# Placing the matmuls' moving operands modulo 256 bytes in a two-layer decoder trunk

## The chip, the cores and the metric

The kernel runs on one core of one Trainium2 chip. The metric is the device time of one execution in microseconds (us); lower is better. Profiles name the engines PE (matmul), PEld (weight load of PE), DVE (vector), ACT (scalar), POOL and SP (which here only issues DMAs). L402 means line 402 of the kernel before.

## What is computed

A decoder trunk of two layers over 528 tokens (512 and 16 meta tokens) of width 1024, in float32. Each layer is half a SwiGLU, a mixer (retention in layer 0, gated linear attention, GLA, in layer 1), and another half SwiGLU; a norm closes the trunk.

```
def swiglu(x, w_in, w_out):
    gate, up = jnp.split(x @ w_in, 2, axis=-1)
    return (jax.nn.silu(gate) * up) @ w_out
...
    for i in range(DEPTH):
        j = i // N_MIXERS
        h = h + 0.5 * swiglu(rmsnorm(h, norm_ffn1[i]), ffn1_w_in[i], ffn1_w_out[i])
        hn = rmsnorm(h, norm_mix[i])
        if i % N_MIXERS == 0:
            mix = retention(hn, ret_w_in[j], ret_head_norm[j], ret_w_out[j])
        else:
            mix = gla(hn, gla_w_in[j], gla_w_gate[j], gla_b_gate[j], gla_head_norm[j], gla_w_out[j])
        h = h + mix
        h = h + 0.5 * swiglu(rmsnorm(h, norm_ffn2[i]), ffn2_w_in[i], ffn2_w_out[i])
    h = rmsnorm(h, final_norm)
    return h[:, N_META:]
```

The hidden width of a SwiGLU is 2816, which is 22 tiles of 128.

## The kernel before

**Products.** Activations lie with the features on the 128 partitions and the tokens along the free axis. Every float32 operand is split in a rounded part `hi` and a rest `lo`, and a product is three matmuls (`mm3`, L402 to L404): weights `hi` with activations `hi`, weights `hi` with activations `lo`, weights `lo` with activations `hi`. The weights (`whi`, `wlo`) are the stationary operand, loaded afresh for each matmul by PEld; the activations are the moving operand, mostly 264 columns (half of the tokens), 256 in the last SwiGLU. In PE's order, a chunk k of 128 input features is three matmuls, with moving operands `hi`, `lo`, `hi`.

**Weights.** `Weights` streams all weights in one planned order: raw tiles by SP's DMA queue, sums of two of them with the help of POOL's, then a split on ACT (L160) and DVE (L161) into two tiles of 512 columns, 2048 bytes a partition, out of 14 in the pool `wsplit`. The split runs four tiles ahead of PE. A chunk k is 128 columns, 512 bytes. Retention has four more such tiles in a pool of its own, `wmore`.

**Units.** Most projections are done two output tiles and two halves of the tokens at a time as a unit (`unit_steps`) of seven passes in place of eight. Each pass multiplies one weight quarter (n chunks, four in the input projections; four or three in the output projections of the SwiGLUs) with one moving operand. In the usual order the moving operands are n11, t1, t2, n21, n3, n22, t4. In an input projection n11, n21 and n22 are slices of `uh` and `ul` (the scaled input, `hi` and `lo`, a tile of eight rows of 528 columns), and n3, t1, t2, t4 are the four quarters of `th` and `tl`, sums of the normed input, four per chunk, each 264 columns. In an output projection all seven lie in one hidden tile `h` per chunk, `hi` and `lo` each with seven slices of 264 columns, in the order n21, n22, n11, n3, t1, t2, t4. The hidden tiles rotate over four buffers (tag `H`).

```
            th, tl = [tp.tile([P, 4, 4, 264], F32R, tag=f"t{i}", name=f"t{i}{me}") for i in "hl"]
...
                    h = hp.tile([P, 2, 7, 264], F32R, tag="H", name=f"h{me}{f}")
...
                    og[h] = [rp.tile([P, 4, T], F32R, tag="v" + i, name=f"og{i}{h}") for i in "hl"]
```

**Memory.** All tiles lie in on-chip memory, one start address for all partitions. Pools are placed behind one another in the order in which they are opened: constants (`const`), the residual stream (`resid`), `upool` with `uh`, `ul` and the norm rows `rb` and `rc`, `tmp` with the scratch tiles, the three weight pools, and then whatever pools a stage opens: in a SwiGLU the hidden tiles, `th` and `tl`, and three scratch tiles; in retention one pool `rp`; in GLA one pool `gp`. A stage's pools are closed at its end, and the next stage's take their place, each tile when the last reader of what lay there is done.

**Norms.** `stats` (L524 to L537) sums the squares by matmul, raises the mean to the power -1/2 on POOL (L535, with a constant tile `half_neg` of eight columns), and `spread` brings the result to all partitions as `rb` (L546). Meanwhile PE runs the next stage's first plain projections, which need `uh` alone.

**Order.** A scheduler of the language sorts each engine's instructions by priority and expected readiness; the text's order decides between equals. The causal mask (`causal`, L356) and a copy of its corner at three places (`ctail`, L359) are used by retention alone.

Of the kernel before, what the change touches and what calls it, by code (L numbers as in the profile page):

```python
# [10 lines left out]
F32 = mybir.dt.float32  # L11
F32R = mybir.dt.float32r
# [40 lines left out]
PW = 512  # L53
AHEAD = 4
# [164 lines left out]
def trunk(ctx, tc, a):  # L219
# [6 lines left out]
    tmp = ctx.enter_context(tc.tile_pool(name="tmp", bufs=2))  # L226
    acc = ctx.enter_context(tc.tile_pool(name="acc", bufs=2, space=bass.MemoryType.PSUM))
    W = Weights(tc, ctx)

# [125 lines left out]
    causal = const.tile([P, P], F32, name="causal")  # L355
    nc.sync.dma_start(causal, a["tri"][1])  # L356
    ctail = const.tile([3 * MR, MR], F32, name="ctail")
    for g in range(3):
        S.copy(ctail[g * MR:(g + 1) * MR], causal[g * MR:(g + 1) * MR, g * MR:(g + 1) * MR])  # L359
# [7 lines left out]
    half_neg = const.tile([P, 8], F32, name="half_neg")  # L367
    V.memset(half_neg, -0.5)
# [6 lines left out]
    rb = upool.tile([P, T], F32, tag="rb", name="rb")  # L375
    rc = upool.tile([P, 8], F32, tag="rc", name="rc")
# [61 lines left out]
    def rsqrt_rows(sq, parts, width, name, finish):  # L438
# [10 lines left out]
        ms = tmp.tile([P, 8], F32, tag="ms", name=f"ms_{name}")  # L449
        V.tensor_scalar(ms[:w, :nj], st[:w, :nj], 1.0 / width, EPS, ALU.mult, ALU.add)  # L450
        r = tmp.tile([P, 8], F32, tag="r", name=f"r_{name}")
        G.tensor_tensor(r[:w, :nj], ms[:w, :nj], half_neg[:w, :nj], ALU.pow)
# [12 lines left out]
    def enter(gcol, by, lag=1, lag2=1):  # L465
# [52 lines left out]
        def stats():  # L518
# [12 lines left out]
            for (b0, w, nb, m), c in zip(by, cols):  # L531
                ms = tmp.tile([P, 8], F32, tag="ms", name=f"ms_{name}{c}")
                V.tensor_scalar(ms[:w, :nb], st[:w, c:c + nb], 1.0 / D, EPS, ALU.mult, ALU.add)
                r = rc[:w, c:c + nb]
                G.tensor_tensor(r, ms[:w, :nb], half_neg[:w, :nb], ALU.pow)  # L535
                n = m // nb
                ins = V.tensor_tensor(dg[:w, b0:b0 + m].rearrange("p (j t) -> p j t", j=nb),  # L537
                                      ident[:w, :n].unsqueeze(1).broadcast_to([w, nb, n]),
                                      r.unsqueeze(2).broadcast_to([w, nb, n]), ALU.mult)
# [102 lines left out]
    def quarters(halves, th, tl):  # L642

        tl = tl if isinstance(tl, list) else [tl[:, k] for k in range(4)]
        wd = width(halves)

        def rhs(what, k):
            if what in ("n11", "n21", "n22"):
                k, (r0, r1) = k + (4 if what[1] == "2" else 0), halves[int(what[2]) - 1]
                return uh[k][:, r0:r1], ul[k][:, r0:r1]  # L650
            i = ("n3", "t1", "t2", "t4").index(what)
            return th[:, k, i, :wd], tl[k][:, i, :wd]
# [4 lines left out]
    def ffn(which, layer, halves, gcol, feed, late=False):  # L657
# [5 lines left out]
        with tc.tile_pool(name=f"h_{me}", bufs=4) as hp, tc.tile_pool(name=f"t_{me}", bufs=1) as tp, \  # L663
                tc.tile_pool(name=f"u_{me}", bufs=3) as up_, psum_pool(4) as pp:
            other["pool"] = pp
            th, tl = [tp.tile([P, 4, 4, 264], F32R, tag=f"t{i}", name=f"t{i}{me}") for i in "hl"]
# [21 lines left out]
            def sums(j):  # L688
                norm(j)
                for i in range(2):  # L690
                    k = 2 * j + i
                    u_sums(up_, f"{me}{k}", halves, normed[j][:, i].rearrange("p h t -> p (h t)"), th[:, k], tl[:, k])
# [17 lines left out]
            def hidden(f, y, part=None):  # L710
# [15 lines left out]
                else:  # L726
                    h = hp.tile([P, 2, 7, 264], F32R, tag="H", name=f"h{me}{f}")
# [248 lines left out]
    def out_last(key, hh, hl, halves, scale):  # L976
# [80 lines left out]
        ms = tmp.tile([P, 8], F32, tag="ms", name="ms_fb")  # L1057
        V.tensor_scalar(ms[:, :2], st[:, :2], 1.0 / D, EPS, ALU.mult, ALU.add)
        r = tmp.tile([P, 8], F32, tag="r", name="r_fb")
        G.tensor_tensor(r[:, :2], ms[:, :2], half_neg[:, :2], ALU.pow)  # L1060
# [15 lines left out]
    def retention(feed):  # L1076
        with tc.tile_pool(name="retp", bufs=1) as rp, tc.tile_pool(name="wmore", bufs=2) as wp, psum_pool(4) as pp:
# [4 lines left out]
            th, tl = [rp.tile([P, 4, 4, 264], F32R, tag=f"t{i}", name=f"rt{i}") for i in "hl"]  # L1082
# [9 lines left out]
            def sums(k):  # L1092
# [7 lines left out]
                u_sums(rp, f"r{k}", HALVES, un.rearrange("p h t -> p (h t)"), th[:, k], tl[:, k])  # L1100
# [17 lines left out]
            def head(h):  # L1118
# [222 lines left out]
                def result():  # L1341

                    og[h] = [rp.tile([P, 4, T], F32R, tag="v" + i, name=f"og{i}{h}") for i in "hl"]
# [64 lines left out]
    def gla(feed):  # L1408
        with tc.tile_pool(name="glap", bufs=1) as gp, psum_pool(2) as pp, \
# [6 lines left out]
            th = gp.tile([P, 4, 4, 264], F32R, tag="th", name="gth")  # L1416
# [5 lines left out]
            def sums(k):  # L1422
# [16 lines left out]
                split(th[:, k, :2], tl[k][:, :2], t01)  # L1439
                split(th[:, k, 2:], tl[k][:, 2:], t23)  # L1440
# [641 lines left out]
```

## Time and profile before

| | |
|---|---|
| median of 3 runs | 2070.59 us (2070.3 to 2073.34) |
| the profiled execution's own time | 2071.41 us |
| its span, first to last instruction | 2069.6 us |
| granted TensorE clock | 0.999 |
| bytes read from main memory | 311.76 MB |
| DMA, mean over the span | 154 GB/s |

A row of the timeline has the start in us, the duration in us, the engine, the line, the operation, what it writes and reads, the shapes and the count. A matmul's duration is longer than the distance to the next one's start, since matmuls overlap; the pace of PE is read from starts. A row of a group has, behind the bar, the busy time and the mean duration in ns, then the idle time before it and what ended it. A row of the windows has the busy time and the count of each engine.

### The profile page before, as it was taken

The page shows a single profiled execution, that of the slowest core. Times are in us where ns is not written, and L with a number is a line of the kernel's source. Part 1 is how long each engine was busy: PE and PEld are TensorE (multiplying, and loading weights), DVE is VectorE, ACT ScalarE, POOL GpSimd, SP SyncE. Part 2 cuts the span into 40 slices and gives each one's busy share as a digit, 9 for nine tenths or more (in the row PEclk, how much of TensorE's full clock was granted, in tenths as well). Part 3 has the DMA queues.
Part 4 walks back from the last instruction along what each step waited for, and adds up shares of the span by engine and source line. Part 5 has one row for each costly group of instructions (what it writes and reads, how often), then busy time and mean ns, then how long its engine had stood idle before and what let it go on. Part 6 is the DMA issues. An engine that isn't in the chain of part 4 may idle for free.

```text
span 2069.6 us, 42946 instructions
## 1 busy us (share of the span) xinstructions
PE 2057.5 (99%) x16335; PEld 2012.9 (97%) x16335; DVE 1790.8 (87%) x3218; ACT 1200.2 (58%) x2365; POOL 208.8 (10%) x181
## 2 busy tenths in 40 slices
PE   9999999999999999999999999999999999999998
PEld 9999999999999999999999999999999988999998
DVE  8988889978686889988889998889897968998886
ACT  5756566554545455656666565666645445666664
POOL 1011111010101000111111011111001000111110
PEclk9999999999999999999999999999999999999999
DMA  7676777355555532776776476677614351687772
GB/s 224 154 193 158 193 185 185 107 144 132 146 132 138 136 104 70 184 191 158 195 188 172 111 180 179 162 197 177 194 57 119 91 165 61 161 214 174 183 179 72
DMA packets 176112, 318.84 MB, mean 154 GB/s; under 512 B 17569, under 2 KB 40737, under 8 KB 175905
## 3 DMA queue, kind: packets, MB, share of 16 engines
q1 hardware_dynamic: 133856, 237.04, 34.6%
q0 software_dynamic: 40896, 75.51, 23.5%
q10 hardware_dynamic: 1152, 3.55, 0.5%
q8 instruction: 128, 2.10, 0.4%
q14 instruction: 80, 0.65, 0.1%
HBM read 311.76 MB, written 4.26 MB: 153 GB/s over the span
## 4 chain that ended last, share of the span: by engine, by line
PE 95%; DVE 2%; ACT 1%; issue 1%; DMA 0%; POOL 0%; SPq 0%; POOLq 0%; ACTq 0%; DVEq 0%
PE po_r L403 2%; PE po_r L402 2%; PE po_r L404 2%; PE Xf20o L402 1%; PE Xf10o L402 1%; PE Xf11o L402 1%; PE Xf10o L404 1%; PE Xf10o L403 1%; PE Xf20o L403 1%; PE Xf20o L404 1%; PE Xf11o L403 1%; PE Xf11o L404 1%; PE lv L1614 1%; PE Xf20u L402 1%; PE Xf11u L402 1%; PE Xf21u L404 1%
## 5 line engine op out<-in xcount | busy, mean ns | idle before, releaser
L160 ACT CAST whi<-raw 128x512 fp32r<-128x512 f32 (+1 forms) x893 | 525.6, 606 | 482.3 <-DVE raw L166 92.2
L161 DVE TENSOR_TENSOR wlo<-raw,whi 128x512 fp32r<-128x512 f32 (+1 forms) x893 | 584.1, 669 | 143.8 <-ACT whi L160 134.7
L160 ACT CAST whi<-pair 128x512 fp32r<-128x512 f32 (+1 forms) x304 | 183.5, 604 | 122.2 <-PE Xf11u L403 7.3
L161 DVE TENSOR_TENSOR wlo<-pair,whi 128x512 fp32r<-128x512 f32 (+1 forms) x304 | 202.0, 664 | 6.4 <-ACT whi L160 5.0
L129 POOL DMA_DIRECT2D pair<-in_f_in x73 | 88.5, 1213 | 725.4 <-DVE wlo L161 313.6
L166 DVE TENSOR_TENSOR raw<-pair,raw 128x512 f32<-128x512 f32 (+1 forms) x146 | 97.3, 667 | 2.6
L168 DVE TENSOR_TENSOR raw<-raw,raw 128x512 f32<-128x512 f32 (+1 forms) x146 | 97.3, 666 | 2.5
L129 POOL DMA_DIRECT2D pair<-in_f_out x44 | 53.2, 1208 | 379.1 <-DVE wlo L161 208.8
L402 PE MATMUL po_r<-ogh,whi 128*128 128x264 f32 x256 | 73.0, 285 | 0.0
L403 PE MATMUL po_r<-ogl,whi 128*128 128x264 f32 x256 | 73.0, 285 | 0.0
L404 PE MATMUL po_r<-ogh,wlo 128*128 128x264 f32 x256 | 72.8, 285 | 0.0
L129 POOL DMA_DIRECT2D pair<-in_ret_in x20 | 24.3, 1215 | 301.8 <-DVE wlo L161 90.7
L402 PE MATMUL Xf20o<-hf,whi 128*128 128x264 f32 x176 | 50.8, 289 | 0.2
L402 PE MATMUL Xf11o<-hf,whi 128*128 128x264 f32 x176 | 50.8, 289 | 0.2
L402 PE MATMUL Xf10o<-hf,whi 128*128 128x264 f32 x176 | 50.8, 289 | 0.2
L403 PE MATMUL Xf10o<-hf,whi 128*128 128x264 f32 x176 | 50.0, 284 | 0.0
L403 PE MATMUL Xf11o<-hf,whi 128*128 128x264 f32 x176 | 50.0, 284 | 0.0
L403 PE MATMUL Xf20o<-hf,whi 128*128 128x264 f32 x176 | 50.0, 284 | 0.0
L404 PE MATMUL Xf10o<-hf,wlo 128*128 128x264 f32 x176 | 49.9, 284 | 0.0
L404 PE MATMUL Xf11o<-hf,wlo 128*128 128x264 f32 x176 | 49.9, 284 | 0.0
L404 PE MATMUL Xf20o<-hf,wlo 128*128 128x264 f32 x176 | 49.9, 284 | 0.0
L402 PEld LDWEIGHTS po_r<-ogh,whi 128*128 128x128 f32 x256 | 48.3, 189 | 0.0
(1007 smaller groups left out, 8523.8 us busy)
## 6 DMA issues: line engine op xcount, KB each, us to landing
raw<-in_f_in SPq DMA_DIRECT2D x277, 256.0 KB, 4.5
pair<-in_f_in SPq DMA_DIRECT2D x150, 256.0 KB, 4.7
pair<-in_f_in POOLq DMA_DIRECT2D x73, 512.0 KB, 6.7
raw<-in_f_out SPq DMA_DIRECT2D x80, 256.0 KB, 3.7
raw<-in_ret_in SPq DMA_DIRECT2D x76, 256.0 KB, 3.3
raw<-in_f_out SPq DMA_DIRECT2D x72, 192.0 KB, 3.2
pair<-in_f_out SPq DMA_DIRECT2D x48, 256.0 KB, 3.9
pair<-in_f_out POOLq DMA_DIRECT2D x24, 512.0 KB, 6.1
```

Source lines behind the costliest of these rows:

```text
L129: nc.gpsimd.dma_start(t, aps[2].unsqueeze(1).broadcast_to([P, 2, n]), accum_op=ALU.add)
L160: self.nc.scalar.copy(hi[:, :n], raw)
L161: V.tensor_sub(lo[:, :n], raw, hi[:, :n].bitcast(F32))
L166: V.tensor_add(s2, self.tiles[c][:, 1], self.tiles[c, "a11"])
L168: V.tensor_add(raw, raw, s2)
L402: nc.tensor.matmul(ps, lhsT=lh, rhs=rh, start=start, stop=False, **kw)
L403: nc.tensor.matmul(ps, lhsT=lh, rhs=rl, start=False, stop=False, **kw)
L404: return nc.tensor.matmul(ps, lhsT=ll, rhs=rh, start=False, stop=stop, **kw)
L1614: nc.tensor.matmul(ps[:, j, J * P:J * P + n], lhsT=Kt[:, j, J * P:(J + 1) * P], rhs=q, start=(J == 0), stop=(J == 3), skip_group_check=True)
```

## The change

1. The SwiGLUs' `th` and `tl` become four tiles each, one per chunk, where the first three are 24 columns (96 bytes) longer than they need to be; the same in retention, and for `th` in GLA.
2. A SwiGLU opens the pool of `th` and `tl` ahead of that of the hidden tiles, with an unused tile of 24 columns at its end.
3. A hidden tile's `hi` and `lo` are 8 columns (32 bytes) longer than they need to be.
4. Retention's output tiles `og` have rows of 544 in place of 528 columns, and an unused tile of 56 columns stands behind the mask.
5. The norm rows `rb` and `rc` and the scratch pool `tmp` move behind the weight pools; the means of squares `ms` get a small pool ahead of them.
6. The mask and the copies of its corner are allocated, loaded and made at the start of retention instead of the kernel's.
7. The exponent -1/2 is one column of `rc`, broadcast, in place of a tile.

The number of matmuls, their shapes and the bytes loaded stay the same.

```diff
--- before.py
+++ after.py
@@ -51,6 +51,9 @@
 BY_JT = ((0, 128, 4, 512), (512, 16, 1, 16))
 BY_P = ((16, 128, 4, 512), (0, 128, 1, 16))
 PW = 512
+SKEW = 4 * 264 + 24
+HW = 7 * 264 + 8
+RSKEW = 56
 AHEAD = 4
 HEAD_START = 300
 
@@ -223,9 +226,11 @@
     const = ctx.enter_context(tc.tile_pool(name="const", bufs=1))
     resid = ctx.enter_context(tc.tile_pool(name="resid", bufs=1))
     upool = ctx.enter_context(tc.tile_pool(name="upool", bufs=1))
-    tmp = ctx.enter_context(tc.tile_pool(name="tmp", bufs=2))
+    small = ctx.enter_context(tc.tile_pool(name="small", bufs=2))
     acc = ctx.enter_context(tc.tile_pool(name="acc", bufs=2, space=bass.MemoryType.PSUM))
     W = Weights(tc, ctx)
+    rows = ctx.enter_context(tc.tile_pool(name="rows", bufs=1))
+    tmp = ctx.enter_context(tc.tile_pool(name="tmp", bufs=2))
 
 
     def ffn_steps(last, late):
@@ -352,11 +357,6 @@
     W.prime()
     ident = const.tile([P, P], F32, name="ident")
     nc.sync.dma_start(ident, a["tri"][0])
-    causal = const.tile([P, P], F32, name="causal")
-    nc.sync.dma_start(causal, a["tri"][1])
-    ctail = const.tile([3 * MR, MR], F32, name="ctail")
-    for g in range(3):
-        S.copy(ctail[g * MR:(g + 1) * MR], causal[g * MR:(g + 1) * MR, g * MR:(g + 1) * MR])
     ones_r = const.tile([P, P], F32R, name="ones")
     V.memset(ones_r.bitcast(F32), 1.0)
     ones = ones_r.bitcast(F32)
@@ -364,16 +364,23 @@
     idle = acc.tile([P, 2, 512], F32, tag="acc", name="idle")[:, 0, :].rearrange("p (n c) -> p n c", c=P)
     for _ in range(IDLE):
         nc.tensor.matmul(idle, lhsT=ones_r, rhs=ones_r.unsqueeze(1).broadcast_to([P, 4, P]), start=True, stop=True)
-    half_neg = const.tile([P, 8], F32, name="half_neg")
-    V.memset(half_neg, -0.5)
     ngains = const.tile([P, NG], F32, name="ngains")
     S.activation(ngains, gains, AF.Copy, scale=-1.0)
 
     uha = upool.tile([P, KD, T], F32R, tag="uh", name="uha")
     ula = upool.tile([P, KD, T], F32R, tag="ul", name="ula")
     uh, ul = [[t[:, d, :] for d in range(KD)] for t in (uha, ula)]
-    rb = upool.tile([P, T], F32, tag="rb", name="rb")
-    rc = upool.tile([P, 8], F32, tag="rc", name="rc")
+    rb = rows.tile([P, T], F32, tag="rb", name="rb")
+    rc = rows.tile([P, 8], F32, tag="rc", name="rc")
+    V.memset(rc[:, 7:8], -0.5)
+
+    def rsqrt(r, ms):
+        G.tensor_tensor(r, ms, rc[:r.shape[0], 7:8].broadcast_to(list(r.shape)), ALU.pow)
+
+    def slices(pool, tag, name):
+
+        return [pool.tile([P, SKEW if k < 3 else 4 * 264], F32R, tag=f"{tag}{k}", name=f"{name}{k}")[:, :4 * 264]
+                .rearrange("p (i t) -> p i t", i=4) for k in range(4)]
 
 
     def urgent():
@@ -446,10 +453,10 @@
         for j in range(nj):
             nc.tensor.matmul(st[:w, j:j + 1], lhsT=sq[:, j * w:(j + 1) * w], rhs=ones[:, 0:1],
                              start=(j == 0), stop=(j == nj - 1), skip_group_check=True)
-        ms = tmp.tile([P, 8], F32, tag="ms", name=f"ms_{name}")
+        ms = small.tile([P, 8], F32, tag="ms", name=f"ms_{name}")
         V.tensor_scalar(ms[:w, :nj], st[:w, :nj], 1.0 / width, EPS, ALU.mult, ALU.add)
         r = tmp.tile([P, 8], F32, tag="r", name=f"r_{name}")
-        G.tensor_tensor(r[:w, :nj], ms[:w, :nj], half_neg[:w, :nj], ALU.pow)
+        rsqrt(r[:w, :nj], ms[:w, :nj])
         dg = tmp.tile([P, T], F32, tag="hf", name=f"dg_{name}")
         V.tensor_tensor(dg[:w, :n].rearrange("p (j t) -> p j t", j=nj),
                         ident[:w, :w].unsqueeze(1).broadcast_to([w, nj, w]),
@@ -529,10 +536,10 @@
                 col += nb
             dg = tmp.tile([P, T], F32, tag="hf", name=f"dg_{name}")
             for (b0, w, nb, m), c in zip(by, cols):
-                ms = tmp.tile([P, 8], F32, tag="ms", name=f"ms_{name}{c}")
+                ms = small.tile([P, 8], F32, tag="ms", name=f"ms_{name}{c}")
                 V.tensor_scalar(ms[:w, :nb], st[:w, c:c + nb], 1.0 / D, EPS, ALU.mult, ALU.add)
                 r = rc[:w, c:c + nb]
-                G.tensor_tensor(r, ms[:w, :nb], half_neg[:w, :nb], ALU.pow)
+                rsqrt(r, ms[:w, :nb])
                 n = m // nb
                 ins = V.tensor_tensor(dg[:w, b0:b0 + m].rearrange("p (j t) -> p j t", j=nb),
                                       ident[:w, :n].unsqueeze(1).broadcast_to([w, nb, n]),
@@ -641,7 +648,6 @@
 
     def quarters(halves, th, tl):
 
-        tl = tl if isinstance(tl, list) else [tl[:, k] for k in range(4)]
         wd = width(halves)
 
         def rhs(what, k):
@@ -649,7 +655,7 @@
                 k, (r0, r1) = k + (4 if what[1] == "2" else 0), halves[int(what[2]) - 1]
                 return uh[k][:, r0:r1], ul[k][:, r0:r1]
             i = ("n3", "t1", "t2", "t4").index(what)
-            return th[:, k, i, :wd], tl[k][:, i, :wd]
+            return th[k][:, i, :wd], tl[k][:, i, :wd]
 
         return rhs
 
@@ -660,10 +666,11 @@
         me = f"{which}{layer}"
         (a0, a1), (b0, b1) = halves
         wd = a1 - a0
-        with tc.tile_pool(name=f"h_{me}", bufs=4) as hp, tc.tile_pool(name=f"t_{me}", bufs=1) as tp, \
+        with tc.tile_pool(name=f"t_{me}", bufs=1) as tp, tc.tile_pool(name=f"h_{me}", bufs=4) as hp, \
                 tc.tile_pool(name=f"u_{me}", bufs=3) as up_, psum_pool(4) as pp:
             other["pool"] = pp
-            th, tl = [tp.tile([P, 4, 4, 264], F32R, tag=f"t{i}", name=f"t{i}{me}") for i in "hl"]
+            th, tl = [slices(tp, f"t{i}", f"t{i}{me}") for i in "hl"]
+            tp.tile([P, 24], F32, tag="skew", name=f"skew{me}")
             rhs_in = quarters(halves, th, tl)
             H, normed = {}, {}
             groups = GROUPS if feed else LAST_GROUPS
@@ -689,7 +696,7 @@
                 norm(j)
                 for i in range(2):
                     k = 2 * j + i
-                    u_sums(up_, f"{me}{k}", halves, normed[j][:, i].rearrange("p h t -> p (h t)"), th[:, k], tl[:, k])
+                    u_sums(up_, f"{me}{k}", halves, normed[j][:, i].rearrange("p h t -> p (h t)"), th[k], tl[k])
 
             def renorm():
                 for h, r0, r1 in ((0, a0, a1), (1, a0, a1), (1, b0, b1)):
@@ -724,7 +731,8 @@
                     t_sums(t, None, None, y[:, 0])
                     split(hi[:, 6], lo[:, 6], t[:, 3])
                 else:
-                    h = hp.tile([P, 2, 7, 264], F32R, tag="H", name=f"h{me}{f}")
+                    h = hp.tile([P, 2, HW], F32R, tag="H", name=f"h{me}{f}")[:, :, :7 * 264]
+                    h = h.rearrange("p i (q t) -> p i q t", q=7)
                     t = up_.tile([P, 4, 264], F32, tag="su", name=f"tt{me}h{f}")[:, :, :wd]
                     hi, lo = h[:, 0, :, :wd], h[:, 1, :, :wd]
                     if part is None:
@@ -1054,10 +1062,10 @@
         with tc.issue_after(ins.ins):
             for d in range(KD - 4, KD):
                 turn(d)
-        ms = tmp.tile([P, 8], F32, tag="ms", name="ms_fb")
+        ms = small.tile([P, 8], F32, tag="ms", name="ms_fb")
         V.tensor_scalar(ms[:, :2], st[:, :2], 1.0 / D, EPS, ALU.mult, ALU.add)
         r = tmp.tile([P, 8], F32, tag="r", name="r_fb")
-        G.tensor_tensor(r[:, :2], ms[:, :2], half_neg[:, :2], ALU.pow)
+        rsqrt(r[:, :2], ms[:, :2])
         for b in range(2):
             for j in range(2):
                 ys = (tmp.tile([P, T], F32, tag="hf", name=f"yb{j}{b}") if j else
@@ -1079,7 +1087,13 @@
             other["pool"] = pp
             (a0, a1), (b0, b1) = HALVES
             wd = a1 - a0
-            th, tl = [rp.tile([P, 4, 4, 264], F32R, tag=f"t{i}", name=f"rt{i}") for i in "hl"]
+            th, tl = [slices(rp, f"t{i}", f"rt{i}") for i in "hl"]
+            causal = rp.tile([P, P], F32, tag="causal", name="causal")
+            nc.sync.dma_start(causal, a["tri"][1])
+            ctail = rp.tile([3 * MR, MR], F32, tag="ctail", name="ctail")
+            for g in range(3):
+                S.copy(ctail[g * MR:(g + 1) * MR], causal[g * MR:(g + 1) * MR, g * MR:(g + 1) * MR])
+            rp.tile([P, RSKEW], F32, tag="skew", name="rskew")
             rhs_u = quarters(HALVES, th, tl)
             og, normed, tabs = {}, {}, {}
 
@@ -1097,7 +1111,7 @@
                 for i in range(2):
                     m = k + 4 - 4 * i
                     V.scalar_tensor_tensor(un[:, i], x[m], ngains[:, G_MIX + m:G_MIX + m + 1], rb, ALU.mult, ALU.mult)
-                u_sums(rp, f"r{k}", HALVES, un.rearrange("p h t -> p (h t)"), th[:, k], tl[:, k])
+                u_sums(rp, f"r{k}", HALVES, un.rearrange("p h t -> p (h t)"), th[k], tl[k])
 
             def renorm(r0, r1):
                 for k in range(0, KD, 2):
@@ -1340,7 +1354,7 @@
 
                 def result():
 
-                    og[h] = [rp.tile([P, 4, T], F32R, tag="v" + i, name=f"og{i}{h}") for i in "hl"]
+                    og[h] = [rp.tile([P, 4, T + 16], F32R, tag="v" + i, name=f"og{i}{h}")[:, :, :T] for i in "hl"]
                     og[h] = [[t[:, m, :] for m in range(4)] for t in og[h]]
 
                 rope("q")
@@ -1413,7 +1427,7 @@
             spilt = [dp_.tile([P, 2, T], F32, tag=f"x{k}", name=f"spill{k}") for k in range(4)]
             for k in range(4):
                 nc.sync.dma_start(spilt[k], xs[k])
-            th = gp.tile([P, 4, 4, 264], F32R, tag="th", name="gth")
+            th = slices(gp, "th", "gth")
             tl, normed = [], []
 
             def two(tag, name):
@@ -1436,8 +1450,8 @@
                 V.scalar_tensor_tensor(t23[:, 0], mid[:, 0], -1.0, t01[:, 1], ALU.mult, ALU.subtract)
                 V.scalar_tensor_tensor(t23[:, 1], un[:, :wd], -1.0, t23[:, 0], ALU.mult, ALU.subtract)
                 tl.append(resid.tile([P, 4, 264], F32R, tag=f"x{k}", name=f"gtl{k}"))
-                split(th[:, k, :2], tl[k][:, :2], t01)
-                split(th[:, k, 2:], tl[k][:, 2:], t23)
+                split(th[k][:, :2], tl[k][:, :2], t01)
+                split(th[k][:, 2:], tl[k][:, 2:], t23)
 
             def renorm():
 
```

## The prediction

> **What bounds the kernel now.** I read the page's head and busy shares first, then the chain that ended last.
>
> ```profile
> span 2069.6 us, 42946 instructions
> PE 2057.5 (99%) x16335; PEld 2012.9 (97%) x16335; DVE 1790.8 (87%) x3218; ACT 1200.2 (58%) x2365; POOL 208.8 (10%) x181
> PEclk9999999999999999999999999999999999999999
> PE 95%; DVE 2%; ACT 1%; issue 1%; DMA 0%; POOL 0%; SPq 0%; POOLq 0%; ACTq 0%; DVEq 0%
> ```
>
> PE is never out of work, its clock is granted in full, and 95% of the chain is PE. Only two things can shorten such a kernel: fewer matmuls, of which this change removes none, or a shorter distance in time from one matmul's start to the next's. So I went to the timeline of PE and read starts. The first stretch is one unit of the SwiGLU input projection, `Xf20u`: seven passes (an eighth row opens the next unit), each of 12 matmuls of 264 columns. The first row of each pass is shown, and the last pass by each of its four weight chunks.
>
> ```profile
> 960.09 0.28 PE L402 MATMUL Xf20u<-uha,whi 128*128 128x264 f32 x1
> ...
> 961.54 0.29 PE L402 MATMUL QZf20u<-thf,whi 128*128 128x264 f32 x1
> ...
> 963.01 0.28 PE L402 MATMUL Xf20u<-thf,whi 128*128 128x264 f32 x1
> ...
> 964.47 0.28 PE L402 MATMUL QZf20u<-uha,whi 128*128 128x264 f32 x1
> ...
> 965.94 0.28 PE L402 MATMUL Xf20u<-thf,whi 128*128 128x264 f32 x1
> ...
> 967.39 0.28 PE L402 MATMUL QZf20u<-uha,whi 128*128 128x264 f32 x1
> ...
> 968.84 0.29 PE L402 MATMUL Xf20u<-thf,whi 128*128 128x264 f32 x1
> ...
> 969.22 0.28 PE L402 MATMUL Xf20u<-thf,whi 128*128 128x264 f32 x1
> ...
> 969.58 0.29 PE L402 MATMUL Xf20u<-thf,whi 128*128 128x264 f32 x1
> ...
> 969.96 0.28 PE L402 MATMUL Xf20u<-thf,whi 128*128 128x264 f32 x1
> ...
> 970.32 0.28 PE L402 MATMUL Xf20g<-uha,whi 128*128 128x264 f32 x1
> ```
>
> The passes take 1.45, 1.47, 1.46, 1.47, 1.45, 1.45 and 1.48 us, 10.23 us for 84 matmuls or 121.8 ns each. Nothing waits inside; still, equal work differs. The last pass, quarter t4, goes 0.38, 0.36, 0.38, 0.36 us by threes: 126.7, 120.0, 126.7, 120.0 ns a matmul. What differs between the chunks is the address.
>
> **Addresses.** Pools lie behind one another in the order in which they are opened, each tile rounded up to 32 bytes a partition; that is read from the code. A weight tile has 2048 bytes and a chunk 512, so in the units all weights of the main pool have one place modulo 256. I call "distance" the moving operand's start minus the weights', modulo 256. Before, from `uh` to the weights lie 2 x 16896 + 2144 + 10688 + 14336 + 12288 = 73248 bytes, so `uh` stands at -32, or 224; each k adds 2112 bytes, or 64, the second token half 1056, or 32. The hidden tiles and `th` start whole multiples of 256 behind the weights, at 0; a quarter adds 32, a k of `th` 4224 bytes, or 128. So in t4 (quarter 3) the chunks stand at 96, 224, 96, 224: **distance 96 costs 126.7 ns, 224 costs 120.0**. The other quarters alternate between 0 and 128 (n3, 1.45 us, 120.8 ns), 32 and 160 (t1, 1.47, 122.5), 64 and 192 (t2, 1.46, 121.7). Starts are read to 0.01 us, which is 0.8 ns a matmul over a pass: these three are coarse, the 6.7 ns of t4 isn't.
>
> The second stretch is an output unit, whose moving operands are the hidden tiles in four buffers:
>
> ```profile
> 888.53 0.28 PE L402 MATMUL Xf20o<-hf,whi 128*128 128x264 f32 x1
> ...
> 889.97 0.28 PE L402 MATMUL QZf20o<-hf,whi 128*128 128x264 f32 x1
> ...
> 891.44 0.29 PE L402 MATMUL Xf20o<-hf,whi 128*128 128x264 f32 x1
> ...
> 892.90 0.28 PE L402 MATMUL QZf20o<-hf,whi 128*128 128x264 f32 x1
> ...
> 898.75 0.28 PE L402 MATMUL Xf20o<-hf,whi 128*128 128x264 f32 x1
> ```
>
> 10.22 us for 84, 121.7 ns each. Before, a buffer is 14784 bytes (-64) and `lo` stands 7392 bytes (-32) behind `hi`, so all eight distances mix. The first pass (n11) has `hi` at 192, 64, 0, 128 and takes 1.44 us; the fourth (n21) has 128, 0, 192, 64 and takes 1.47. The same four distances in another order differ by 2.5 ns a matmul: order counts about as much as the set. That is the weakness of what follows.
>
> **The change part by part.** *Quarters.* `th` now starts 2144 + 10624 bytes behind the weights' end, at 224; a k steps by 4320 bytes (-32), `tl` lies 17184 bytes (+32) behind. So `hi` is at 224 + 32 x quarter - 32 x k, from 128 round to 64: never 96. `lo` is 32 further and meets 96 once in 16 (t4, k = 0). Every pass takes one distance of each of the four pairs above, 224 for the last: (120.8 + 122.5 + 121.7 + 120.0) / 4 = 121.25 ns; the four `lo` matmuls of t4 cost 122.9. 44 x 121.25 + 4 x 122.9 = 5.83 us a unit against 1.47 + 1.46 + 1.45 + 1.48 = 5.86. The units:
>
> ```profile
> 0.00:2069.60 2069.60, 458.84 (x3720) 453.41 (x3720) 97.08 (x100) 84.58 (x100) 1.00 0.59 154
> 0.00:2069.60 2069.60, 473.39 (x2400) 386.21 (x2400) 19.55 (x16) 16.41 (x16) 1.00 0.59 154
> ```
>
> These are the whole span with the instructions of `hf`, then of `thf`, alone: 3720 and 2400 matmuls. A unit reads `thf` 32 times, so 75 units in the SwiGLUs; by the plan retention has 20, GLA 7: 102 x -0.033 = **-3.4 us**. *`uh`.* Between it and the weights now lie 33792 + 64 + 26624 = 60480 bytes: 192. The halves change sets: n11 and n21 go from {224, 32, 96, 160} (1.45 and 1.47 us) to {0, 64, 128, 192} (n22, 1.45), n22 the other way: -0.011 us a unit, **-1.1 us**; plain projections read both halves and keep the sum. *Hidden tiles.* `lo` now stands 7424 bytes (0) behind `hi`, a buffer is 14848 (0): one distance all through a pass, 128, 160, 192, 224, 0, 32, 64 by quarter. By the values above 850 / 7 = 121.4 against 121.7: 3720 x -0.24 ns = **-0.9 us**. *Retention's output tiles* step by 128 instead of 64, with `lo` 128 from `hi` as before:
>
> ```profile
> L402 PE MATMUL po_r<-ogh,whi 128*128 128x264 f32 x256 | 73.0, 285 | 0.0
> ```
>
> 256 such, and as many of L403 and L404; no row isolates a distance there. A nanosecond either way bounds it at 0.8 us; I take 0.
>
> *Moved mask.* The causal mask's load and its three ACT copies leave the start and go to the entrance of retention.
>
> ```profile
> L359 ACT COPY ctail<-causal x3: 211/213/218, 18.8 to 19.3; 32x32 f32<-32x32 f32 x3
> L356 SPq DMA_DIRECT2D causal<-in_tri x1: 327/327/327, 11.8 to 11.8; - x1
> 355.99 0.33 SPq L1090 DMA_DIRECT2D ropeq<-in_rope  x1
> ...
> 356.88 23.26 SPq L132 DMA_DIRECT2D raw<-in_ret_in  x10
> ...
> 361.89 0.62 ACT L160 CAST whi<-raw 128x512 fp32r<-128x512 f32 x1 [2.06 <-PE pq L403]
> ```
>
> At the start the copies' 0.64 us lie beside PE's first projections: 0 gained. In retention the DMA stands ahead of the two table loads on SP, whose buffers are released at the same end of the last output unit; behind it are those tables and ten weight loads, 0.33 us later. The copies fit into ACT's 2.06 us of idleness, which PE itself ends. If ACT held them until the load has landed, weight splits behind them would wait; four split tiles ahead, of 1.45 us each, cover that. Bounds: 0 to +2 us; I take 0. *Norm row and scratch:* the exponent becomes one column broadcast.
>
> ```profile
> L535 POOL TENSOR_TENSOR rc<-ms_n,half_neg 128x4 f32<-128x4 f32 (+2 forms) x11 | 10.9, 1000 | 85.6 <-DVE ms_n L533 85.6
> ```
>
> The same operation, 1.0 us, off PE's path behind plain projections. POOL alone writes `rc` after the start, so no new wait. No row shows a broadcast; half to double is -0.5 to +1 us a call, hidden: 0.
>
> The sum is -5.4 us. Since order moved equal sets by as much as sets differ, I take the middle between nothing and all of it: -2.7 us. The profiled execution's span is 2069.6, its run 2071.4; against the median, 2070.6 - 2.7 = **2067.9 us**.
>
> **The rivals.** *All of it or more:* the places act one by one; 2065.2. For it: t4's clean alternation. The far end is every moved matmul at 120.0 (102 x 84 + 3720 = 12288 x 1.8 = -22 us, 2048.5), which a set of seven distances can't reach. *Nothing:* no reader waits for another, order averages out; 2070.6. Against it: t4. The Trainium skill says so ("SBUF — State Buffer", Who interferes with whom): PE has two independent read ports, one for moving operands and one for weights, and never waits. By that rule the sum would be 0; the trace disagrees, with 126.7 beside 120.0 ns. *Slower, by constant distance:* in a hidden pass the stall no longer alternates; a bad distance holds for the whole pass. If three of seven passes stand at t4's 126.7 instead of some 121.7, that is 3/7 x 3720 x 5 ns = +8.0, less half of the 4.5 us of `th` and `uh`: 2070.6 + 5.8 = 2076.4. With one pass of seven it is -2.2 + 2.7, no change; it decides from three. Against it: 96 is left out.
>
> **How the numbers follow.** This kernel tells 0.2%, 4.1 us, from no change. Forecast, between -4.1 and 0: 0.40. All or more (-4.1 to some -12): 0.37. Nothing (within 1 us): 0.07. Slower: 0.16. So faster 0.37, same 0.47, slower 0.16. The forecast's own range is 2066 to 2071; with the other cases, less a tenth on each side, 2060 to 2075.5.
>
> **What would show it.** Right: t4's passes fall from 1.48 to 1.46 us or less, n11 and n21 of `uh` to 1.45, hidden passes are flat from chunk to chunk, and counts and waits stay. Wrong: passes of quarter t1 or of the output at distance 32 or 160 above 1.48 us; a wait of PE for a split after 356 us; a longer norm step on POOL.

## The result and the profile after

The changed kernel takes 2073.48 us (median of 22 runs, 2071.49 to 2076.93), the kernel before 2070.45 us beside it (22 runs): a ratio of 1.0014, 95% interval 1.0008 to 1.0021. Measured twice more beside before it gave 1.0011 (1.0002 to 1.0020) and 1.0012 (1.0003 to 1.0021). So it is slower, by 2.0 to 3.0 us between the medians, within the 0.2% that the prediction called no change, above the forecast's own range of 2066 to 2071 us, and on the other side of 0 than the -2.7 us forecast.

The head of the page of the changed kernel, its busy shares, the clock and the chain:

```profile
span 2072.3 us, 42947 instructions
PE 2059.4 (99%) x16335; PEld 2013.8 (97%) x16335; DVE 1790.9 (86%) x3218; ACT 1200.7 (58%) x2365; POOL 208.9 (10%) x181
PEclk9999999999999999999999999999999999999999
PE 91%; DVE 4%; DMA 1%; ACT 1%; issue 1%; POOL 0%; SPq 0%; POOLq 0%; DVEq 0%; ACTq 0%
```

The matmul count and the clock are the same, and so is what DVE, ACT and POOL do. PE's work is still most of the chain: 91%, beside 95% in the profile of before, but a second profile of the kernel before also has 91%, and a second one of the changed kernel 96%. So the question stays the one of the prediction: the time from one matmul's start to the next's. This is the unit `Xf20u` in PE's timeline of the changed kernel, the first row of each pass, as it was shown of before:

```profile
960.78 0.29 PE L409 MATMUL Xf20u<-uha,whi 128*128 128x264 f32 x1
...
962.25 0.29 PE L409 MATMUL QZf20u<-thf,whi 128*128 128x264 f32 x1
...
963.71 0.29 PE L409 MATMUL Xf20u<-thf,whi 128*128 128x264 f32 x1
...
965.18 0.29 PE L409 MATMUL QZf20u<-uha,whi 128*128 128x264 f32 x1
...
966.65 0.29 PE L409 MATMUL Xf20u<-thf,whi 128*128 128x264 f32 x1
...
968.13 0.28 PE L409 MATMUL QZf20u<-uha,whi 128*128 128x264 f32 x1
...
969.60 0.28 PE L409 MATMUL Xf20u<-thf,whi 128*128 128x264 f32 x1
...
971.04 0.29 PE L409 MATMUL Xf20g<-uha,whi 128*128 128x264 f32 x1
```

The unit takes 10.26 us instead of 10.23. In order (n11, t1, t2, n21, n3, n22, t4) the passes take 1.47, 1.46, 1.47, 1.47, 1.48, 1.47, 1.44 us; before it was 1.45, 1.47, 1.46, 1.47, 1.45, 1.45, 1.48. Quarter t4 did lose its bad chunks, as forecast. But all three passes of `uh` and quarter n3 became slower. The output unit, first and last row, went the forecast way, from 10.22 to 10.20 us:

```profile
889.19 0.29 PE L409 MATMUL Xf20o<-hf,whi 128*128 128x264 f32 x1
...
899.39 0.29 PE L409 MATMUL Xf20o<-hf,whi 128*128 128x264 f32 x1
```

One unit read to 0.01 us is coarse, so from here on I use means: of the 53 input units of 264 columns in the SwiGLUs, those in which no matmul starts over 142 ns after the one ahead (46 to 50 of them in each profile). Starts are taken from the trace, which has them in whole ns where the timeline shows 0.01 us; a pass is the start of its first matmul to that of the next pass's first. Before, such a unit takes 10.228 us (standard deviation 0.004), after, 10.256.

### The profile page after: what moved, and what is told of

Its sections match the earlier page's. It is cut to its first block, busy times and chain, and to the rows that moved or that the text cites. A ratio compares the mean times of both kernels' runs of the same rounds, so it can differ in the third digit from the quotient of the medians.

```text
span 2072.3 us, 42947 instructions
## 1 busy us (share of the span) xinstructions
PE 2059.4 (99%) x16335; PEld 2013.8 (97%) x16335; DVE 1790.9 (86%) x3218; ACT 1200.7 (58%) x2365; POOL 208.9 (10%) x181
## 4 chain that ended last, share of the span: by engine, by line
PE 91%; DVE 4%; DMA 1%; ACT 1%; issue 1%; POOL 0%; SPq 0%; POOLq 0%; DVEq 0%; ACTq 0%
PE po_r L411 2%; PE po_r L409 2%; PE po_r L410 2%; DVE wlo L164 1%; PE Xf11u L409 1%; PE Xf11u L411 1%; PE Xf11u L410 1%; PE lv L1628 1%; PE Xf21o L409 1%; PE Xf21u L409 1%; PE Xf21u L410 1%; PE Xf20u L409 1%; PE Xf21u L411 1%; PE Xf20u L410 1%; PE Xf20u L411 1%
## 5 line engine op out<-in xcount | busy, mean ns | idle before, releaser
L163 ACT CAST whi<-pair 128x512 fp32r<-128x512 f32 (+1 forms) x304 | 183.5, 604 | 122.2 <-PE Xf11u L410 7.4
L410 PEld LDWEIGHTS po_r<-ogl,whi 128*128 128x128 f32 x256 | 48.3, 189 | 0.0
```

The source lines that it names most:

```text
L163: self.nc.scalar.copy(hi[:, :n], raw)
L410: nc.tensor.matmul(ps, lhsT=lh, rhs=rl, start=False, stop=False, **kw)
```

## The experiments

Two theories stood against each other, and a third beside them. **Place**, the prediction's own: each distance modulo 256 has its price, and prices add up. **Sequence**: the price of a matmul depends on the addresses of its neighbours in PE's order too, so a place has no price of its own. **Entrance**: the loss lies in single late weight loads at the entrances of stages, where the changed kernel's first profile showed some 2 us more of pauses.

All times below, each ratio against before measured in the same sitting (11 runs against 33):

```
run               median us  before   ratio, 95% interval        span of the profile
e1_before_again   2070.08    2070.50  0.9999 (0.9991 to 1.0008)  2070.1
e2_after_again    2072.47    2070.50  1.0011 (1.0002 to 1.0020)  2072.4
e3_mask           2070.96    2070.50  1.0004 (0.9995 to 1.0013)  2069.3
e4_uh192          2071.45    2070.50  1.0007 (0.9998 to 1.0016)  2069.0
e5_hidden         2071.03    2070.64  1.0002 (0.9993 to 1.0011)  2069.1
e6_quarters       2071.10    2070.64  1.0004 (0.9995 to 1.0013)  2069.5
e7_even           2070.34    2070.64  0.9999 (0.9990 to 1.0007)  2068.7
e9_shift          2071.39    2070.64  1.0002 (0.9993 to 1.0010)  2069.5
e10_uh_quarters   2073.79    2070.07  1.0018 (1.0009 to 1.0027)  2070.9
e11_after_uh224   2070.78    2070.07  1.0005 (0.9996 to 1.0013)  2070.3
e12_hidden0       2070.37    2070.07  1.0004 (0.9995 to 1.0013)  2069.6
e13_after_third   2072.26    2070.07  1.0012 (1.0003 to 1.0021)  2070.2
```

Only the changed kernel and e10 differ from before by more than their interval. And the mean input unit of each profile, in us, split in its three passes of `uh` and its four of the quarters:

```
run               uh at  quarters    uh passes  quarters' passes  unit
before            224    as before   4.371      5.857             10.228
e1_before_again   224    as before   4.371      5.857             10.228
e3_mask           224    as before   4.371      5.857             10.228
e9_shift          224    as before   4.372      5.857             10.229
e4_uh192          192    as before   4.377      5.857             10.234
e6_quarters       224    as after    4.368      5.845             10.213
e11_after_uh224   224    as after    4.369      5.846             10.215
e10_uh_quarters   192    as after    4.405      5.852             10.258
after             192    as after    4.404      5.852             10.256
e2, e13 (after)   192    as after    4.404/405  5.852/851         10.256/256
e7_even           224    one a pass  4.383      5.817             10.200
```

**The two kernels again.** No edit.

> The kernel before, unchanged, against itself: a second profile and the size of a difference that means nothing. Theory 'pace' (the places of the moving operands set the distance between matmul starts, the same in every execution): ratio 1.000, within 0.0006; starts of passes that wait for nothing repeat to 0.01 us. Theory 'entrance' (what was gained or lost lies in single waits of PE for weights that arrive late): the wait in front of the fourth SwiGLU, 1.61 us of ACT for a raw weight load in the first profile, comes back at 1.61 us if it is fixed by the program, and moves by a us if it is chance.

> The changed kernel, unchanged, a second profile: +3.0 us again (2073.5). Theory 'entrance': ACT's wait for the raw load at the fourth SwiGLU is again about 2.8 us and not 1.6 us, and PE's gaps add up to some 2.4 us more than before. Theory 'pace': the gaps are chance; the sum of PE's start distances without gaps is again +0.4 us against before, made of +1.3 us for the normalized input, -1.3 us for the hidden tiles and +0.4 us for the quarters, and the rest of the 3 us has to be found elsewhere.

> The changed kernel, a third profile beside the two kernels above on the same chip: 2072.5 to 2073.5. What all three profiles of it have in common and no kernel with the input at 224 has is the program's; single waits of PE that come in one profile and not in the others (0.6 to 1.2 us at the entrances of the fourth SwiGLU and of GLA so far) are chance.

The changed kernel took 2072.47 and 2072.26 us this time, a little under the 2073.5 and the 2072.5 to 2073.5 expected. The pace repeats and the entrances don't. The units agree to 0.001 us over three profiles of the changed kernel. The wait of ACT for a raw weight load in front of the fourth SwiGLU changes from execution to execution; it is the one in brackets in ACT's timeline, first in the two profiles of before (in the second the profile puts it down to DVE), then in the three of after:

```profile
1124.85 0.62 ACT L160 CAST whi<-raw 128x512 fp32r<-128x512 f32 x1 [1.61 <-DMA raw<-in_f_in]
```

```profile
1126.21 0.62 ACT L160 CAST whi<-raw 128x512 fp32r<-128x512 f32 x1 [2.66 <-DVE wlo L161]
```

```profile
1127.22 0.62 ACT L163 CAST whi<-raw 128x512 fp32r<-128x512 f32 x1 [2.81 <-DMA raw<-in_f_in]
```

```profile
1125.12 0.62 ACT L163 CAST whi<-raw 128x512 fp32r<-128x512 f32 x1 [1.60 <-DMA raw<-in_f_in]
```

```profile
1125.48 0.63 ACT L163 CAST whi<-raw 128x512 fp32r<-128x512 f32 x1 [1.81 <-DMA raw<-in_f_in]
```

1.6 and 2.7 us before, 2.8, 1.6 and 1.8 after: chance, in both kernels. The theory "entrance" falls as an account of the loss. This wait had been the largest single difference between the first two profiles (about 1 us of it came out at PE).

**The moved mask alone.**

```diff
-    causal = const.tile([P, P], F32, name="causal")
-    nc.sync.dma_start(causal, a["tri"][1])
...
+            causal = rp.tile([P, P], F32, tag="causal", name="causal")
+            nc.sync.dma_start(causal, a["tri"][1])
...
+            rp.tile([P, 32], F32, tag="skew", name="rskew")
```

> Before, with the causal mask and its corner loaded inside retention, all distances of moving operands as before. By the step of the prediction: 0 (0 to +2 us), 2070.5. If the moved load and copies, or the 640 bytes that they free in front of everything, carry the slowdown: +2 to +3 us, 2072.5 to 2073.5, with longer waits of PE after 356 us.

1.0004, which is no change. In the changed kernel the copies wait a little for the load, in time that ACT has (ACT's timeline), so the step at the entrance is hidden as forecast:

```profile
359.72 0.67 ACT L1095 COPY ctail<-causal 32x32 f32<-32x32 f32 x3 [0.28 <-DMA causal<-in_tri]
```

But far behind it, in the third SwiGLU, something moved. ACT's timeline of before and of e3, then PE's of e3:

```profile
1000.67 0.51 ACT L160 CAST whi<-raw 128x384 fp32r<-128x384 f32 x1 [0.32 <-ACT suf20o L620]
```

```profile
1000.20 0.51 ACT L160 CAST whi<-raw 128x384 fp32r<-128x384 f32 x1 [0.61 <-ACT suf20o L615]
```

```profile
1001.85 0.28 PE L399 MATMUL QZf20o<-hf,wlo 128*128 128x264 f32 x1
...
1002.30 0.39 PE L397 MATMUL Xf20o<-hf,whi 128*128 128x264 f32 x1 [0.17 <-DVE x L877]
```

The same cast waits 0.29 us longer behind the same copy, DVE's split of `lo` and its reading of PE's result follow later, and PE stands for 0.45 us from start to start (1001.85 to 1002.30) instead of the 0.15 of before (1002.61 to 1002.76). This pause of 0.43 to 0.45 us is in all eleven profiles with the mask inside retention, and in none of the three with it at the start (two of before, and e12, 0.15 us). Two more places do the same (0.12 to some 0.27 us near 1346 us, 0.12 to 0.30 near 1895). Together that is 0.6 us, and 0.8 with the distances right behind the last two, which grow by 0.1 each; the step "0" didn't have it, and it is below what the timing of e3 can tell. Why the cast starts later isn't settled: the copy named had ended long before, and the instructions have the same order and the same kinds of waits there.

**The input alone.** e3 with one line more, which puts `uh` at 192:

```diff
+    tmp.tile([P, 8], F32, tag="pad", name="pad", bufs=1)
```

> The kernel of the moved mask, with one pad of 32 bytes that puts the normalized input at 192 instead of 224 and leaves every other large operand's distance alone. By the prediction's step: -1.1 us against before, 2069.4. By the spacing in the profile of the change (121.5 to 122.0 ns for the high part, 121.9 to 121.7 for the low one): +1.3 us, 2071.8, with matmuls of 264 columns of the high part at 122.0 ns. If only gaps count: no change, 2070.5.

Neither -1.1 nor +1.3 us came in the pace. The `uh` passes go from 4.371 to 4.377 us, some +0.4 us over 75 units, which the time (1.0007, from 0.9998) can't tell from nothing; and matmuls of 264 columns of the high part take 121.5 ns in the mean, the same as at 224; in the changed kernel the same input at the same 192 takes 122.0. So the 122.0 isn't the price of 192. The small sum hides larger moves: n11 goes from 1.453 to 1.465 us and n22 from 1.447 to 1.462, which are the changed kernel's values already, while n21 falls from 1.471 to 1.449. Outside the units, the plain projections on `uh` take 0.6 us less in all. Matmul by matmul nearly everything changed: between two kernels with equal distances (before and e3), the times from start to start of the matmuls with the same number correlate with 0.85 for `uha` and 0.93 for `thf`; between e3 and e4 with -0.06 and 0.40. `thf` had not moved at all against its weights. Only its neighbours had.

**The same distances, 256 bytes on.** e3 with a pad of 64 columns (256 bytes) in the same place.

> The kernel of the moved mask, with the normalized input 256 bytes further from the weights, so that every distance modulo 256 is as before. If modulo 256 is all there is of the address: uha, ula, thf, tlf and hf repeat to 0.1 ns in their means, matmul by matmul as between two runs of before (121.5, 121.9, 121.8, 122.2, 121.8), and the time is the moved mask's 2071.0. If a longer distance counts too: uha and ula change matmul by matmul, by some ns either way, with a mean within 0.5 ns of before, and the passes that follow them change too.

Nothing changes: 10.229 us a unit, the means of uha, ula, thf, tlf and hf within 0.1 ns, correlations with e3 of 0.88, 0.90, 0.92, 0.84 and 0.82, as between two profiles with equal distances. For the input, whole multiples of 256 bytes don't count. That part of the address model holds. Counting modulo 128 would not do: in t4 of before, 96 and 224 are equal modulo 128 and take 126.7 and 120.0 ns in turn.

**The hidden tiles alone.**

```diff
+HW = 7 * 264 + 8
...
-                    h = hp.tile([P, 2, 7, 264], F32R, tag="H", name=f"h{me}{f}")
+                    h = hp.tile([P, 2, HW], F32R, tag="H", name=f"h{me}{f}")[:, :, :7 * 264]
+                    h = h.rearrange("p i (q t) -> p i q t", q=7)
```

(and two pads of 128 bytes, in front of the hidden tiles and behind them, that set their start to 128 and leave `th` at 0.)

> The kernel of the moved mask, with the hidden tiles alone laid out as in the change (one distance through a pass, 128 to 64 by quarter); input, quarters and retention stand as before. Theory 'place' (each distance modulo 256 has its own price): the prediction's -0.9 us and the -1.3 us that the spacing of hf showed in the changed kernel, so hf at 121.5 ns, and 2069.7 to 2070.1 against the moved mask's 2071.0; thf and uha at 121.8 and 121.5 ns as before. Theory 'sequence' (a matmul's pace comes from the addresses of its neighbours as well, so it has no price of its own): hf moves by under 1 us in either sign, and only passes next to hidden ones move with it.

The mean output unit (16 to 18 without a pause) falls from 10.225 to 10.196 us, with 10.196 in the changed kernel; input units keep their time within 0.002 us. `hf` has 121.5 ns at 264 columns instead of 121.8, -0.8 us over its matmuls; at 256 columns 118.0, where profiles with the old tiles have 118.1 to 118.4. This part does alone what it does in the change: passes of the output projection have mostly each other as neighbours. Both theories allow that, so this run doesn't choose between them; the time, 2071.03 us, shows no gain.

**The hidden tiles from another start.** Before with the same edit and no pads: 0 to 192 by quarter, the mask at the start.

> The kernel before, with the hidden tiles at one distance through a pass and nothing else: 0, 32, 64 to 192 by quarter (the change had 128 round to 64), the mask stays at the start. Theory 'sequence': hidden passes have only each other as neighbours, so their gain comes again in about the size of the other start, -0.3 to -1.1 us, 2069.5 to 2070.3, with uha, ula, thf and tlf as before matmul by matmul. Theory 'place': it trades the pass at 224 for one at 96; if 96 costs what it cost quarter t4 (126.7 ns), a seventh of 3720 matmuls loses 5 ns, +2.6 us, 2072 or more.

Both theories missed. The output unit takes 10.244 us, 0.019 more than before, where the start at 128 had gained 0.029. One distance a pass is no merit in itself; and a distance of 96 for a whole pass does not cost 126.7 ns either: that pass, n3, takes 1.463 us, 121.9 ns a matmul, and 1.471 before.

**The quarters alone.** The slices of the change in e3, and a front pad of 56 columns that gives them the change's distances:

```diff
+            tp.tile([P, 56], F32, tag="front", name=f"front{me}")
+            th, tl = [slices(tp, f"t{i}", f"t{i}{me}") for i in "hl"]
```

> The kernel of the moved mask, with the quarters alone at the distances of the change in SwiGLU, GLA and (but for an eighth of its reads) retention. Prediction's step: -3.4 us, 2067.6. Theory 'place' with the changed kernel's spacing: high part -1.1 us, low part +1.4 us, so about +0.3 us, 2071.3, with thf at 121.4 and tlf at 122.8 ns of 264 columns. Theory 'sequence': thf and tlf land elsewhere than in the changed kernel, since the normalized input between them stands at another distance, and the sum is within 1 us of 0.

The unit falls to 10.213 us, 0.015 of the forecast 0.033. `thf` takes 121.6 and `tlf` 122.0 ns, not the 121.4 and 122.8 of the changed kernel: the same distances, another neighbour. In the last SwiGLU, whose units have 256 columns, the same quarters cost time: 9.944 us a unit instead of 9.922.

**Both together.** e6 with e4's pad.

> The kernel of the moved mask, with the input at 192 and the quarters at the distances of the change, hidden tiles as before: the two parts that were tried alone, together. Theory 'place': their effects add up; the spacing of uha, ula, thf and tlf alone summed to about -0.2 us for the input and -1.0 us for the quarters, so -1.2 us against the moved mask, 2069.8, with uha at 121.7 and tlf at 122.0 ns. Theory 'sequence': the two stand next to each other in every unit, so together they do what they do in the changed kernel: uha 122.0, ula 121.7, thf 121.4, tlf 122.8 ns, some +1.1 us against the moved mask, 2072.1.

This is the decisive run. +0.006 for the input and -0.015 for the quarters should make 10.219 us; the unit takes 10.258, as in the changed kernel (10.256). uha, ula, thf and tlf have 122.0, 121.7, 121.4 and 122.9 ns, the changed kernel's 122.0, 121.7, 121.4 and 122.8. The time is 2073.79 us, 1.0018. The 0.039 us beyond the sum lie in n21: 1.471 us before, 1.449 with the input alone, 1.458 with the quarters alone, so 1.436 by the sum, and 1.477 with both. In the other six passes the differences from the sum cancel to 0.002 us. First and last row of `Xf20u` in e10, 10.26 us, then in e6, 10.21:

```profile
960.05 0.29 PE L405 MATMUL Xf20u<-uha,whi 128*128 128x264 f32 x1
...
970.31 0.29 PE L405 MATMUL Xf20g<-uha,whi 128*128 128x264 f32 x1
```

```profile
958.90 0.28 PE L404 MATMUL Xf20u<-uha,whi 128*128 128x264 f32 x1
...
969.11 0.28 PE L404 MATMUL Xf20g<-uha,whi 128*128 128x264 f32 x1
```

**The change with the input back at 224.**

```diff
+    small.tile([P, 56], F32, tag="pad", name="pad", bufs=1)
...
-    ngains = const.tile([P, NG], F32, name="ngains")
+    ngains = const.tile([P, G_FIN], F32, name="ngains")
```

> The changed kernel with the normalized input back at 224 and all else at the change's distances (the table of negative gains is cut to its used columns to make room). Theory 'sequence': uha, ula, thf and tlf as in the kernel with the quarters alone (121.7, 121.2, 121.6, 122.0 ns), hidden tiles 121.5: some 2.1 us less spacing than the changed kernel, 2070.4 beside 2072.5. Theory 'entrance' (the slowdown is late weight loads or the order of pools): as the changed kernel, 2072.5. Prediction's step for the input: giving up its -1.1 us, 2073.6.

2070.78 us, 1.5 us less than the changed kernel beside it (2072.26) and no different from before (1.0005). The unit takes 10.215 us, e6's value. A shift of one tile by 32 bytes, counted modulo 256, undoes the slowdown, and all other distances of the change stay.

**One distance a pass.** e3 with rows of 272 columns:

```diff
-            th, tl = [tp.tile([P, 4, 4, 264], F32R, tag=f"t{i}", name=f"t{i}{me}") for i in "hl"]
+            th, tl = [tp.tile([P, 4, 4, 272], F32R, tag=f"t{i}", name=f"t{i}{me}") for i in "hl"]
```

> The kernel of the moved mask, with quarters of 272 columns a row: one distance through a pass, 0, 64, 128 and 192 by quarter, high and low alike, and none at 32, 96, 160, 224. Averages by distance in the profile of before: thf and tlf 121.6 at 0 and 64, 121.2 at 128, 120.6 at 192, against 121.9 over all distances. Theory 'place': -0.7 ns for 102 units of 48 matmuls, -3.4 us, 2067.6. Theory 'sequence': the averages don't carry over; the four passes are no faster than before by more than 0.3 ns a matmul, and the time stays at 2071. The exponent of the norm row is one broadcast column here, as in the change: 0.

The quarters' passes gain 0.040 us, 0.8 ns a matmul, about the sum by place, and more than the 0.3 ns that "sequence" allowed; but the three passes of `uh`, whose places stayed, lose 0.012, and the averages by distance didn't carry over. `thf` at 192, the cheapest of the four before (120.0 ns), is the dearest here (122.0), and at 64 it has 122.1 ns before, 120.4 here, 122.9 in e6 and 118.6 in the changed kernel. Plainest of all is t4, where all four chunks now stand at 192, high and low alike: they take 123.1, 126.5, 120.3 and 120.0 ns a matmul. One place has no one price even inside a pass. The unit is the shortest of all, 10.200 us; the time, 2070.34 us, can't be told from before (0.9999). No version measured beats the kernel before by more than its interval.

## Why the prediction missed

**The bound** was read rightly. PE stayed at 99%, no wait of a microsecond or more comes in all profiles of the changed kernel and not before, and the main question was the pace.

**Addresses.** Counting the distance modulo 256 holds for the input (e9). The step that failed is the next one, "distance 96 costs 126.7 ns, 224 costs 120.0", and with it the sentence that every pass takes one distance of each of the four pairs, (120.8 + 122.5 + 121.7 + 120.0) / 4: it takes the price of a distance out of one sequence and puts it in another. The profile of before already spoke against that. Its passes n11 and n21 stand at the same four distances in the same order, 224, 32, 96, 160, high and low alike, and the prediction itself read 1.45 and 1.47 us for them. And pass n11 has its third chunk at 96 as well; these are the starts of its third and fourth chunk in the timeline of before:

```profile
960.81 0.28 PE L402 MATMUL Xf20u<-uha,whi 128*128 128x264 f32 x1
...
961.17 0.28 PE L402 MATMUL Xf20u<-uha,whi 128*128 128x264 f32 x1
```

0.36 us for three, 120 ns at distance 96; over the units without a pause it is 120.4 ns, in n21 125.0 and in t4 126.4. I had rested on t4's clean alternation and not looked for a second pass with the same distance. (Calling the 6.7 ns of t4 not coarse was wrong as well, since 0.01 us over three matmuls is 3.3 ns; the means, 126.4 and 120.0, bear it out.) The weakness was named (equal sets in another order differ by 2.5 ns), but I let it only halve the sum. It should have taken the sign away. What the runs show in its place is that a matmul's pace depends on the addresses of the stretch around it: the same distances have other prices beside other neighbours (e4, e6, e7), and two moves together do what neither does alone (e10, e11). No rule came out of it that forecasts a pace; "sequence" was wrong in its own forecasts for e7 and e12, and why n21 depends on the quarters while n11 and n22 hardly do stays open.

**Quarters, -3.4 us.** Alone -0.012 us a unit in their own passes, a third of the -0.033; in the change -0.005. Retention's and GLA's units, 27 of the 102, grew by 0.2 us in all. t4 fell as said, from 1.478 to 1.449 us in the mean unit, but n3 rose from 1.457 to 1.478.

**`uh`, -1.1 us.** The passes n11 and n21 were to reach 1.45; they went from 1.453 to 1.465 and from 1.471 to 1.477 us, and n22 from 1.447 to 1.462. That is +0.033 us a unit instead of -0.011, and it is the loss. n11 and n22 are longer with the input alone as well (e4: 1.465 and 1.462), but there n21 makes up for it with 1.449, the 1.45 that was forecast; the new quarters take that away. Of the 75 units in the SwiGLUs 19 have 256 columns, where the mean goes from 9.922 to 9.961 us; the start distances of all 75, pauses left out, sum to +2.2 us. **Plain projections, "keep the sum".** They didn't: -0.6 us, in all five profiles with the input at 192 and in no other.

**Hidden tiles, -0.9 us.** Right in sign and nearly in size: -0.7 us at 264 columns and some -0.4 at 256 in the changed kernel. Right for too general a reason, as e12 shows.

**Retention's output tiles, 0 (0.8 us either way).** The high part went from 122.3 to 123.3 ns, the low one from 122.2 to 121.0: +0.5 and -0.3 us for 512 and 256 matmuls, within the bound.

**The mask, 0 (0 to +2 us).** Hidden at the entrance; +0.8 us at three later pauses that no step named. **Norm row and scratch, 0.** In the changed kernel's groups the same 1000 ns on POOL:

```profile
L378 POOL TENSOR_TENSOR rc<-ms_n,rc 128x4 f32<-128x4 f32 (+2 forms) x11 | 10.9, 1000 | 86.0 <-DVE ms_n L540 86.0
```

The sum after the fact: the SwiGLUs' input units +2.2, hidden tiles -1.1, plain projections -0.6, the other units +0.2, output tiles +0.2, the mask's pauses +0.8, and two pauses of 0.1 to 0.2 us that come in the five profiles with the input at 192 and in no other (near 59 and 409 us), +0.3: +2.0 us, of the 2.0 to 3.0 measured. So the pace alone makes some +0.9 us of it: without the gain of the hidden tiles the loss would be larger. What is left is below what a ratio's interval (1.3 to 1.9 us either way) can tell.

**The rivals.** *Nothing* (within 1 us) is nearer than the forecast and still off by 1 to 2 us, and its reason, that order averages out, is wrong. The Trainium skill ("SBUF — State Buffer", Who interferes with whom) gives PE two independent read ports and lets it wait for no one. The section is about contention between engines; read, as the prediction did, as a rule on a matmul's own two operands, it leaves no way for the unit to depend on where they lie. It takes 10.200 to 10.258 us by places alone, 0.7 ns a matmul, and repeats to 0.001 us, so the runs disagree with that reading, if by half a per cent; that the two ports collide is not shown by it. *Slower by constant distance* has the sign and not the place: the constant distances gained. *All of it or more* is out. None of the signs of being wrong that the prediction named came with the change (a pass above 1.48 us, a new wait of PE for a weight split in all its profiles, a longer norm step); what failed was a sign of being right, n11 and n21 at 1.45.

## What to carry to other kernels

A difference between equal instructions that repeats in every execution is real, and still no price list: before summing it over thousands of matmuls, look in the same profile for the same condition in another surrounding, and see whether it costs the same there. Parts that share a stretch of work should be tried together as well as alone, since here two parts of +0.006 and -0.015 us made +0.030. And where a change is worth a tenth of a per cent, a second profile of each kernel is needed before any single wait of a microsecond is given a meaning.

## What was not expected of the hardware

Passes of matmuls that wait for nothing repeat to a nanosecond or two in the mean between kernels that share only the distances modulo 256 of that stretch: t4 takes 1.4492 to 1.4497 us in the changed kernel's three profiles and in e10, 1.4609 in e6 and in e11. This fits a state that one matmul hands on to the next, as do the four chunks at one place in e7 (123.1, 126.5, 120.3, 120.0 ns); what that state is isn't shown here. And with a load and three copies moved to 356 to 360 us, a cast on ACT starts 0.29 us later some 640 us behind them; the pause that follows came in every kernel that had them moved, and why is open.
